# A log-sum-exp over 16384 rows: four-row reductions on VectorE, the last row loaded in two pieces, and a second pass in whole-ring operations

## Chip, cores, metric

One core of a Trainium2 chip. Times are device microseconds (us); the kernel before takes 168.85 us (median of 3 runs, 168.8 to 169.13). In the profile PE is TensorE, ACT is ScalarE, DVE is VectorE, SP is SyncE, which issues the DMAs here.

## The reference

```python
x = np.random.randn(32, 512, 1024).astype(np.float32)
def reference(x):
    max_x = np.max(x, axis=-1, keepdims=True)
    return (max_x.squeeze(-1) + np.log(np.sum(np.exp(x - max_x), axis=-1))).astype(np.float32)
```

The input is 67 MB, the output 64 KB. Each of the 128 partitions holds 128 rows of 1024 values ("a row" below is 128x1024, one row per partition, 512 KB).

## The kernel before

It computes ln(sum(exp(x))) without the maximum, checks that every sum lies inside wide bounds, and runs a second, exact pass only if one does not. On this input the second pass is never executed. The parts that matter, with cuts marked:

```python
RING = 48                                  # rows of input that fit in the ring
loads = [16, 16, 16, 16, 13, 10, 9, 7, 6, 5, 4, 3, 2, 2, 1, 1, 1]
ACCUMULATED_FROM = NC - 5                  # NC = 128
FIRST_CHECK = 112
# ... tiles; check(c0, c1, i, last): clamp the sums, count those that changed, add the count by matmul
for size in loads:
    p0 = c0 % RING
    nc.sync.dma_start(out=ring[:, p0 : p0 + size, :], in_=x_rows[:, c0 : c0 + size, :])
    if c0 >= ACCUMULATED_FROM:             # the last 5 rows: exp and sum in one ScalarE instruction
        for r in range(size):
            nc.scalar.activation(out=v, in_=v, func=AF.Exp, accum_out=sumexp[:, c0 + r : c0 + r + 1])
    else:                                  # four rows of exp, then one VectorE sum a row
        for b in range(0, size, 4):
            nc.scalar.activation(out=v, in_=v, func=AF.Exp)
            for r in range(b, b + s):
                nc.vector.scalar_tensor_tensor(out=lo, in0=lo, scalar=1.0, in1=ring[:, p0 + r, H:d],
                    op0=ALU.mult, op1=ALU.add, accum_out=sumexp[:, c0 + r : c0 + r + 1])
    if c0 < FIRST_CHECK <= c0 + size:      # the early ln
        nc.scalar.activation(out=res[:, 0:FIRST_CHECK], in_=sumexp[:, 0:FIRST_CHECK], func=AF.Ln)
        check(0, FIRST_CHECK, 0, False)
    c0 += size
nc.scalar.activation(out=res[:, FIRST_CHECK:NC], in_=sumexp[:, FIRST_CHECK:NC], func=AF.Ln)
nc.sync.dma_start(out=out_view, in_=res)
check(FIRST_CHECK, NC, 1, True)
nc.vector.tensor_copy(out=nbad, in_=count)
outside = nc.values_load(nbad[0:1, 0:1], ...)
with tc.If(outside > 0):                   # the second pass: 16 steps of 8 rows, two slots
    for k, c0 in enumerate(range(0, NC, 8)):
        # ... load 8 rows, negated max of 8 rows, then for each row:
        #     exp with the negated max as bias and the sum as accumulator (128 in all)
    # ... ln, subtract, store
```

## Time and profile before

| | before |
|---|---|
| time, median | 168.85 us |
| span of the profile | 167.0 us |
| last row has landed | 160.24 us |
| ScalarE's last accumulation ends | 162.07 us |
| output has landed | 163.88 us |

From the page: busy tenths in 40 slices of 4.2 us, packets of the instruction queue (packets, MB, share), the chain of waits by engine, and groups of instructions (line, engine, operation, shapes, count, busy us, mean ns, idle time before them and what ended it).

```profile
span 167.0 us, 438 instructions
...
DVE  0000005665077712776066746757737393584810
ACT  3000049990899519992599879989597979879980
...
DMA  7979998999799799989999999999999999999800
...
q14 instruction: 6, 0.05, 0.1%
...
DMA 73%; ACT 20%; DVE 3%; issue 1%; SPq 0%; PE 0%; ACTq 0%
...
L90 DVE SCALAR_TENSOR_TENSOR ring<-ring 128x512 f32<-128x512 f32 x123 | 77.6, 687 | 79.1 <-ACT ring L87 78.9
...
L96 ACT ACTIVATE res<-sumexp 128x112 f32<-128x112 f32 x1 | 0.3, 297 | 1.0 <-DVE ring L90 1.0
```

The DMA row is full to the end of slice 37: input streams without a break, and no compute engine is full all the way. The same from the view by windows (start and end, length, then busy time of PE, PEld, DVE, ACT, POOL, granted clock, share of the DMA engines, GB/s):

```profile
40.00:120.00 80.00, 0.00 (x0) 0.00 (x0) 44.83 (x141) 62.91 (x19) 0.00 (x0) 1.00 0.99 427
...
149.00:162.10 13.10, 0.19 (x2) 0.09 (x2) 6.91 (x26) 13.07 (x14) 0.00 (x0) 1.00 0.71 291
```

At 427 GB/s a row needs 1.23 us. In the last 13 us ScalarE is busy 13.07 of 13.10 us: there it looks like the limit. The timeline shows how it fell behind (start, length, engine, line, operation, in brackets the idle time before it):

```profile
143.01 4.56 ACT L87 ACTIVATE ring<-ring 128x4096 f32<-128x4096 f32 x2 [0.67 <-DMA ring<-in_x_dram]
148.62 0.30 ACT L96 ACTIVATE res<-sumexp 128x112 f32<-128x112 f32 x1 [1.04 <-DVE ring L90]
148.82 3.60 ACT L87 ACTIVATE ring<-ring 128x4096 f32<-128x4096 f32 x1
```

The early ln of 112 columns stands in ScalarE's queue behind the exp of rows 109 to 113 (counted from 0), waits 1.04 us for VectorE's sums of the first three of them, and holds the next exp up. And the end of the kernel:

```profile
160.94 1.04 ACT L80 ACTIVATE ring<-ring 128x1024 f32<-128x1024 f32 x1
161.88 0.18 ACT L80 ACTIVATION_READ_ACCUMULATOR ring<-ring 128x1 f32 x1
162.10 0.21 ACT L102 ACTIVATE res<-sumexp 128x16 f32<-128x16 f32 x1
...
162.34 0.35 SPq L103 DMA_DIRECT2D out_dram<-res  x1
...
162.77 0.14 DVE L105 CAST nbad<-count 1x1 int32<-1x1 f32 x1 [0.28 <-PE count L70]
```

The last work ends at 162.92 us, but the span goes to 167.0. SyncE's own waits in this last stretch (engine and line, what it waited for, us, times, longest; two of five lines) name one cause:

```profile
SPq L103 <- ACT res L102: 19.4, 1, 19.4
SPq L153 <- ACTq L111: 1.0, 1, 1.0
```

The second line: at the end of the program SyncE waited 1.0 us for ScalarE's sequencer at L111, which is the `tc.If`. The trace's records of the sequencers give the detail: ScalarE's compare-and-branch ends at 163.53 us and its next instruction comes at 166.22 us.

### The profile page before, as it was taken

The page shows a single profiled execution, that of the slowest core. Times are in us where ns is not written, and L with a number is a line of the kernel's source. Part 1 is how long each engine was busy: PE and PEld are TensorE (multiplying, and loading weights), DVE is VectorE, ACT ScalarE, POOL GpSimd, SP SyncE. Part 2 cuts the span into 40 slices and gives each one's busy share as a digit, 9 for nine tenths or more (in the row PEclk, how much of TensorE's full clock was granted, in tenths as well). Part 3 has the DMA queues.
Part 4 walks back from the last instruction along what each step waited for, and adds up shares of the span by engine and source line. Part 5 has one row for each costly group of instructions (what it writes and reads, how often), then busy time and mean ns, then how long its engine had stood idle before and what let it go on. Part 6 is the DMA issues. An engine that isn't in the chain of part 4 may idle for free.

```text
span 167.0 us, 438 instructions
## 1 busy us (share of the span) xinstructions
PE 0.4 (0%) x4; PEld 0.2 (0%) x4; DVE 78.8 (47%) x254; ACT 116.3 (70%) x48; POOL 0.2 (0%) x4
## 2 busy tenths in 40 slices
PE   0000000000000000000000000000000000000000
PEld 0000000000000000000000000000000000000000
DVE  0000005665077712776066746757737393584810
ACT  3000049990899519992599879989597979879980
POOL 0000000000000000000000000000000000000000
DMA  7979998999799799989999999999999999999800
GB/s 251 502 345 408 502 487 361 408 502 424 330 502 504 345 408 502 471 361 424 408 434 446 423 432 432 446 424 433 402 428 428 441 410 432 417 424 416 357 9 22
DMA packets 2598, 67.22 MB, mean 402 GB/s; under 512 B 288, under 2 KB 416, under 8 KB 800
## 3 DMA queue, kind: packets, MB, share of 16 engines
q1 hardware_dynamic: 2592, 67.18, 93.9%
q14 instruction: 6, 0.05, 0.1%
HBM read 67.11 MB, written 0.07 MB: 402 GB/s over the span
## 4 chain that ended last, share of the span: by engine, by line
DMA 73%; ACT 20%; DVE 3%; issue 1%; SPq 0%; PE 0%; ACTq 0%
DMA ring<-in_x_dram 73%; ACT ring L87 17%; ACT ring L80 3%; DVE ring L90 2%; SPq L76 0%; PE count L70 0%; DVE clamped L66 0%; DVE clamped L62 0%; DVE nbad L105 0%; ACTq L87 0%; ACT res L96 0%
## 5 line engine op out<-in xcount | busy, mean ns | idle before, releaser
L87 ACT ACTIVATE ring<-ring 128x4096 f32<-128x4096 f32 (+3 forms) x35 | 109.4, 3190 | 44.2 <-DMA ring<-in_x_dram 42.2
L90 DVE SCALAR_TENSOR_TENSOR ring<-ring 128x512 f32<-128x512 f32 x123 | 77.6, 687 | 79.1 <-ACT ring L87 78.9
L90 DVE DVE_READ_ACCUMULATOR ring<-ring 128x1 f32 x123 | 10.0, 81 | 0.0
L80 ACT ACTIVATE ring<-ring 128x1024 f32<-128x1024 f32 x5 | 5.2, 1039 | 0.0
L62 DVE TENSOR_SCALAR clamped<-sumexp 128x112 f32<-128x112 f32 (+1 forms) x2 | 0.4, 192 | 3.8 <-ACT ring L80 3.8
L57 ACT ACT_TABLE_LOAD x1 | 1.3, 1283 | 0.7 <-PEq L142 0.7
L96 ACT ACTIVATE res<-sumexp 128x112 f32<-128x112 f32 x1 | 0.3, 297 | 1.0 <-DVE ring L90 1.0
L80 ACT ACTIVATION_READ_ACCUMULATOR ring<-ring 128x1 f32 x5 | 0.9, 185 | 0.0
L70 PE MATMUL count<-ones,bad 128*1 128x1 f32 x4 | 0.4, 164 | 162.4 <-DVE clamped L66 162.4
L66 DVE SCALAR_TENSOR_TENSOR clamped<-clamped,sumexp 128x112 f32<-128x112 f32 (+1 forms) x2 | 0.5, 226 | 0.1
L58 DVE MEMSET ones<- 128x1 f32 x1 | 0.1, 59 | 0.8 <-PEq L142 0.8
L70 PEld LDWEIGHTS count<-ones,bad 128*1 128x1 f32 x4 | 0.2, 80 | 162.5 <-DVE clamped L66 162.5
L105 DVE CAST nbad<-count 1x1 int32<-1x1 f32 x1 | 0.1, 145 | 0.3 <-PE count L70 0.3
L102 ACT ACTIVATE res<-sumexp 128x16 f32<-128x16 f32 x1 | 0.2, 215 | 0.0
L66 DVE DVE_READ_ACCUMULATOR clamped<-clamped,sumexp 128x1 f32 x2 | 0.2, 82 | 0.0
L142 POOL MEMSET const-uint8-127<- 128x1 uint8 x1 | 0.1, 102 | 0.0
L142 POOL MEMSET const-bfloat16-1.0<- 128x1 bf16 x1 | 0.1, 101 | 0.0
L142 POOL MEMSET const-float32-0.0<- 128x1 f32 x1 | 0.1, 98 | 0.2 <-issue 0.2
L142 POOL MEMSET const-float32-1.0<- 128x1 f32 x1 | 0.1, 98 | 0.0
## 6 DMA issues: line engine op xcount, KB each, us to landing
ring<-in_x_dram SPq DMA_DIRECT2D x1, 6656.0 KB, 39.7
ring<-in_x_dram SPq DMA_DIRECT2D x1, 5120.0 KB, 38.1
ring<-in_x_dram SPq DMA_DIRECT2D x1, 4608.0 KB, 41.3
ring<-in_x_dram SPq DMA_DIRECT2D x1, 3584.0 KB, 39.0
ring<-in_x_dram SPq DMA_DIRECT2D x1, 3072.0 KB, 40.5
ring<-in_x_dram SPq DMA_DIRECT2D x1, 2560.0 KB, 40.8
ring<-in_x_dram SPq DMA_DIRECT2D x1, 2048.0 KB, 42.2
ring<-in_x_dram SPq DMA_DIRECT2D x2, 1024.0 KB, 44.9
```

The source lines that it names most:

```text
L57: nc.scalar.preload_act_table_set("natural_log_exp_and_others")
L58: nc.vector.memset(ones, 1.0)
L62: nc.vector.tensor_scalar(out=clamped[:, c0:c1], in0=sumexp[:, c0:c1], scalar1=LOW, scalar2=HIGH, op0=ALU.max, op1=ALU.min,)
L66: nc.vector.scalar_tensor_tensor(out=clamped[:, c0:c1], in0=clamped[:, c0:c1], scalar=0.0, in1=sumexp[:, c0:c1], op0=ALU.bypass, op1=ALU.n ...
L70: nc.tensor.matmul(count, lhsT=bad[:, i : i + 1], rhs=ones, start=i == 0, stop=last)
L80: nc.scalar.activation(out=v, in_=v, func=AF.Exp, accum_out=sumexp[:, c0 + r : c0 + r + 1])
L87: nc.scalar.activation(out=v, in_=v, func=AF.Exp)
L90: nc.vector.scalar_tensor_tensor(out=lo, in0=lo, scalar=1.0, in1=ring[:, p0 + r, H:d], op0=ALU.mult, op1=ALU.add, accum_out=sumexp[:, c0 + ...
L96: nc.scalar.activation(out=res[:, 0:FIRST_CHECK], in_=sumexp[:, 0:FIRST_CHECK], func=AF.Ln)
L102: nc.scalar.activation(out=res[:, FIRST_CHECK:NC], in_=sumexp[:, FIRST_CHECK:NC], func=AF.Ln)
L105: nc.vector.tensor_copy(out=nbad, in_=count)
L142: nc = _bacc.Bacc("TRN2", target_bir_lowering=False, num_devices=1)
```

## The change

Its intent: fewer VectorE instructions for the bulk rows, a shorter tail (only a quarter of the last row is left to do after the last byte lands; the two sums are joined because ln can add a per-partition bias before the logarithm), an early ln that waits for nothing recent, and a second pass of few, large instructions. Cut to its core:

```diff
-    loads = [16, 16, 16, 16, 13, 10, 9, 7, 6, 5, 4, 3, 2, 2, 1, 1, 1]
+    loads = [(16, "R")] * 5 + [(13, "T"), (10, "T"), (7, "T"), (5, "T"), (4, "T"), (3, "T"), (2, "T")]
+    loads += [(1, "A")] * 3
+    LAST = NC - 1
+    SPLIT = 3 * d // 4
+    EARLY = 80
@@ bulk rows
+            if how == "R":
+                nc.vector.reduce_sum(out=sumexp[:, c0 + b : c0 + b + s], in_=v, axis=AX.X)
+                continue
@@ early ln
-        if c0 < FIRST_CHECK <= c0 + size:
-            nc.scalar.activation(out=res[:, 0:FIRST_CHECK], in_=sumexp[:, 0:FIRST_CHECK], func=AF.Ln)
-            check(0, FIRST_CHECK, 0, False)
+        if size == 10:
+            nc.scalar.activation(out=res[:, 0:EARLY], in_=sumexp[:, 0:EARLY], func=AF.Ln)
@@ last row
+    load(p0, LAST, 1, 0, SPLIT)
+    load(p0, LAST, 1, SPLIT, d)
+    exp_sum(ring[:, p0, 0:SPLIT], LAST)
+    nc.scalar.activation(out=res[:, EARLY:LAST], in_=sumexp[:, EARLY:LAST], func=AF.Ln)
+    check(0, LAST, 0)
+    exp_sum(ring[:, p0, SPLIT:d], NC)
+    nc.scalar.activation(
+        out=res[:, LAST:NC], in_=sumexp[:, NC : NC + 1], func=AF.Ln, bias=sumexp[:, LAST:NC]
+    )
@@ second pass
-    with tc.If(outside > 0):
-        STEP = 8
-        for k, c0 in enumerate(range(0, NC, STEP)):
-            ...                       # load 8 rows, max of 8, 8 exps with bias and accumulator
+    with tc.If(outside > 0, preferred_fallthrough_block=False):
+        for c0 in range(0, NC, RING):
+            s = min(RING, NC - c0)
+            load(0, c0, s)
+            nc.vector.tensor_reduce(out=neg, in_=v, op=ALU.max, axis=AX.X, negate=True)
+            nc.vector.tensor_add(out=v, in0=v, in1=neg[:, :, None].to_broadcast([P, s, d]))
+            nc.scalar.activation(out=v, in_=v, func=AF.Exp)
+            nc.vector.reduce_sum(out=sumexp[:, c0 : c0 + s], in_=v, axis=AX.X)
```

("R": four rows by one reduction. "T": one pair-sum a row, as before. "A": exp with accumulator.) ScalarE's order in the built program differs in one place from the source: the ln of 47 columns comes ahead of the exp of the 768-column piece.

More of the change, by code (lines that the diff above doesn't have):

```diff
@@ L38 @@
     RING = 48
-    loads = [16, 16, 16, 16, 13, 10, 9, 7, 6, 5, 4, 3, 2, 2, 1, 1, 1]
-    ACCUMULATED_FROM = NC - 5
-    FIRST_CHECK = 112
-    assert sum(loads) == NC
+    loads = [(16, "R")] * 5 + [(13, "T"), (10, "T"), (7, "T"), (5, "T"), (4, "T"), (3, "T"), (2, "T")]
[3 more added lines that the diff above has]
+    EARLY = 80
+    assert sum(size for size, _ in loads) == LAST
     big = ctx.enter_context(tc.tile_pool(name="big", bufs=1))
@@ L48 @@
     ring = big.tile([P, RING, d], fp32, name="ring")
-    sumexp = stats.tile([P, NC], fp32, name="sumexp")
+    sumexp = stats.tile([P, NC + 1], fp32, name="sumexp")
     res = stats.tile([P, NC], fp32, name="res")
     clamped = stats.tile([P, NC], fp32, name="clamped")
-    bad = stats.tile([P, 2], fp32, name="bad")
+    bad = stats.tile([P, 4], fp32, name="bad")
     ones = stats.tile([P, 1], fp32, name="ones")
@@ L58, with add_to_count, check @@
     nc.vector.memset(ones, 1.0)
-    def check(c0, c1, i, last):
+    def add_to_count(i, last=False):
+        nc.tensor.matmul(count, lhsT=bad[:, i : i + 1], rhs=ones, start=i == 0, stop=last)
+    def check(c0, c1, i):
         nc.vector.tensor_scalar(
@@ L69, in check @@
         )
-        nc.tensor.matmul(count, lhsT=bad[:, i : i + 1], rhs=ones, start=i == 0, stop=last)
-    c0 = 0
-    for size in loads:
-        p0 = c0 % RING
-        assert p0 + size <= RING
-        nc.sync.dma_start(out=ring[:, p0 : p0 + size, :], in_=x_rows[:, c0 : c0 + size, :])
-        if c0 >= ACCUMULATED_FROM:
-            for r in range(size):
-                v = ring[:, p0 + r, :]
-                nc.scalar.activation(
-                    out=v, in_=v, func=AF.Exp, accum_out=sumexp[:, c0 + r : c0 + r + 1]
-                )
-        else:
-            for b in range(0, size, 4):
-                s = min(4, size - b)
-                v = ring[:, p0 + b : p0 + b + s, :]
-                nc.scalar.activation(out=v, in_=v, func=AF.Exp)
-                for r in range(b, b + s):
-                    lo = ring[:, p0 + r, 0:H]
-                    nc.vector.scalar_tensor_tensor(
-                        out=lo, in0=lo, scalar=1.0, in1=ring[:, p0 + r, H:d],
-                        op0=ALU.mult, op1=ALU.add,
-                        accum_out=sumexp[:, c0 + r : c0 + r + 1],
-                    )
-        if c0 < FIRST_CHECK <= c0 + size:
-            nc.scalar.activation(
-                out=res[:, 0:FIRST_CHECK], in_=sumexp[:, 0:FIRST_CHECK], func=AF.Ln
-            )
-            check(0, FIRST_CHECK, 0, False)
-        c0 += size
@@ L102, with load, exp_sum @@
-    nc.scalar.activation(out=res[:, FIRST_CHECK:NC], in_=sumexp[:, FIRST_CHECK:NC], func=AF.Ln)
-    nc.sync.dma_start(out=out_view, in_=res)
-    check(FIRST_CHECK, NC, 1, True)
+        add_to_count(i)
+    def load(p0, c0, size, k0=0, k1=d):
+        nc.sync.dma_start(
+            out=ring[:, p0 : p0 + size, k0:k1], in_=x_rows[:, c0 : c0 + size, k0:k1]
+        )
+    def exp_sum(v, c):
+        nc.scalar.activation(out=v, in_=v, func=AF.Exp, accum_out=sumexp[:, c : c + 1])
+    c0 = 0
+    p0 = 0
@@ new lines @@
+    for size, how in loads:
+        if p0 + size > RING:
+            p0 = 0
+        load(p0, c0, size)
+        for b in range(0, size, 4):
+            s = min(4, size - b)
+            v = ring[:, p0 + b : p0 + b + s, :]
+            if how == "A":
+                exp_sum(v, c0 + b)
+                continue
+            nc.scalar.activation(out=v, in_=v, func=AF.Exp)
+            if how == "R":
+                nc.vector.reduce_sum(out=sumexp[:, c0 + b : c0 + b + s], in_=v, axis=AX.X)
+                continue
+            for r in range(b, b + s):
+                lo = ring[:, p0 + r, 0:H]
+                nc.vector.scalar_tensor_tensor(
+                    out=lo, in0=lo, scalar=1.0, in1=ring[:, p0 + r, H:d],
+                    op0=ALU.mult, op1=ALU.add,
+                    accum_out=sumexp[:, c0 + r : c0 + r + 1],
+                )
+        c0 += size
+        p0 += size
+        if size == 10:
+            nc.scalar.activation(out=res[:, 0:EARLY], in_=sumexp[:, 0:EARLY], func=AF.Ln)
@@ new lines @@
+    load(p0, LAST, 1, 0, SPLIT)
[6 more added lines that the diff above has]
+        out=res[:, LAST:NC], in_=sumexp[:, NC : NC + 1], func=AF.Ln, bias=sumexp[:, LAST:NC]
+    )
+    nc.sync.dma_start(out=out_view, in_=res)
+    for i, c in ((1, LAST), (2, NC)):
+        nc.vector.tensor_scalar(
+            out=bad[:, 3:4], in0=sumexp[:, c : c + 1],
+            scalar1=LOW, scalar2=HIGH, op0=ALU.max, op1=ALU.min,
+        )
+        nc.vector.tensor_tensor(
+            out=bad[:, i : i + 1], in0=bad[:, 3:4], in1=sumexp[:, c : c + 1], op=ALU.not_equal
+        )
+        add_to_count(i, last=i == 2)
@@ L108 @@
         nbad[0:1, 0:1], min_val=0, max_val=P * NC,
-        skip_runtime_bounds_check_because="a count of sums"
+        skip_runtime_bounds_check_because="a count of sums",
     )
-    with tc.If(outside > 0):
-        STEP = 8
-        for k, c0 in enumerate(range(0, NC, STEP)):
-            p0 = (k % 2) * STEP
-            xt = ring[:, p0 : p0 + STEP, :]
-            neg = clamped[:, c0 : c0 + STEP]
-            nc.sync.dma_start(out=xt, in_=x_rows[:, c0 : c0 + STEP, :])
-            nc.vector.tensor_reduce(out=neg, in_=xt, op=ALU.max, axis=AX.X, negate=True)
-            for r in range(STEP):
-                v = ring[:, p0 + r, :]
-                nc.scalar.activation(
-                    out=v, in_=v, func=AF.Exp, bias=clamped[:, c0 + r : c0 + r + 1],
-                    accum_out=sumexp[:, c0 + r : c0 + r + 1],
-                )
-        nc.scalar.activation(out=res, in_=sumexp, func=AF.Ln)
+    with tc.If(outside > 0, preferred_fallthrough_block=False):
+        for c0 in range(0, NC, RING):
+            s = min(RING, NC - c0)
+            v = ring[:, 0:s, :]
+            neg = clamped[:, c0 : c0 + s]
+            load(0, c0, s)
+            nc.vector.tensor_reduce(out=neg, in_=v, op=ALU.max, axis=AX.X, negate=True)
+            nc.vector.tensor_add(out=v, in0=v, in1=neg[:, :, None].to_broadcast([P, s, d]))
+            nc.scalar.activation(out=v, in_=v, func=AF.Exp)
+            nc.vector.reduce_sum(out=sumexp[:, c0 : c0 + s], in_=v, axis=AX.X)
+        nc.scalar.activation(out=res, in_=sumexp[:, 0:NC], func=AF.Ln)
         nc.vector.tensor_sub(out=res, in0=res, in1=clamped)
```

## The prediction

> **What bounds it.** The windows view has the DMA engines 98 to 100% busy to 149 us: the loads never starve. By the trace's landing times a row of 128x1024 takes 1.21 to 1.24 us, and the last lands at 160.24 us. So 160 of 167.0 us is the input stream, which the change does not shorten. The chain of waits is 73% DMA, then from 143 us ScalarE: it never catches up again. In the timeline it loses 1.0 us at 148.6, where the early ln waits for VectorE sums just issued ("ACT res <- DVE ring 1.0"), then runs without a gap to 162.07, 1.8 us after the last landing. The last 5.0 us are ln (0.21), output DMA (1.5 to landing) and the end of the program. In it ScalarE passes its compare-and-branch at 163.53 and executes its next instruction only at 166.22; SyncE was through at 165.27. The instruction queue fetched 8 KB at 165.2. The Trainium skill ("Runtime: NRT & Kernel Launch", Instruction fetch mechanics) says that a taken branch whose target is outside the current window forces a fetch; this stall of 2.7 us agrees.
>
> **The change, costed.**
> 1. 80 rows in 20 reductions of 128x4096 in place of 80 sums of 512 pairs. A sum costs 0.614 us start to start, 2.46 per four rows. The skill ("VectorE: DVE Perf Modes", tier table) gives tensor_reduce one element per cycle only; from 0.96 GHz I estimate 4.3 to 4.4 us per four rows. That is slower than now, but under the 4.84 us in which four rows land: I estimate the fourth load issued at 44.4 us instead of 39.87, still 17 us before the queue runs dry. VectorE busy rises to about 115 us: 0 us on the path.
> 2. The early ln (80 columns) waits only for sums finished long before: removes the 1.0 us wait.
> 3. Fewer accumulated rows at 1.04 us, more in batches at 0.88: -0.2 us. The last row in two pieces costs ScalarE 0.83 + 0.40 instead of 1.04, and ln of 47 (0.25) now comes after the loads: about +0.3 us. ScalarE is still behind: by my sum it ends its accumulation at 161.0 to 162.0 (before 162.07). So the split gains almost nothing.
> 4. The last checks are as long as before.
> 5. Second pass: never executed, but 128 exps become 3, so the branch passes over few instructions. I expect ScalarE's stall to go, and SyncE to set the end: -1.0 to -1.4 us.
> 6. Fewer VectorE instructions: the fetch at 123.8 us, after which one DMA engine landed 0.95 us later, moves or goes; between -0.9 and 0.
>
> **Sum.** ScalarE's end -0.5, branch -1.3: about -1.8 us; 168.85 to 167.0 us, 80% range 166.1 to 168.3. Under 165.5 would need 3.4 us: faster 4%, same 95%, slower 1%.
>
> **What would show it.** Reductions of 4.3 us and no starved DMA slice; no wait of the early ln; ScalarE without a gap over the last 30 us; under 0.5 us between ScalarE's branch and next instruction; from the end of the last accumulation to the end 3.6 us instead of 5.0.
>
> **What would make it wrong.** Reductions at half rate (VectorE becomes the limit, over 180 us); a branch that still fetches (then 168.3); an instruction fetch that delays a DMA engine at the very end; pieces of 1 KB per partition that land late; ScalarE waiting for its own accumulator between the last exp and ln.

## The result

| | before | after |
|---|---|---|
| time, median | 168.82 us (4 runs, 168.63 to 169.13) | 166.32 us (4 runs, 166.22 to 166.67) |
| span of the profile | 167.0 us | 164.6 us |
| last row has landed | 160.24 us | 159.60 us |
| ScalarE's last accumulation ends | 162.07 us | 161.25 us |
| output has landed | 163.88 us | 163.15 us |
| ScalarE: end of last branch, next instruction | 163.53, 166.22 us | 163.25, 163.38 us |

The ratio is 0.9854 (95% interval 0.9833 to 0.9875), 2.5 us. Ratios in this document are from runs of a kernel and of the kernel before in the same rounds, and not quite the ratio of the medians; where microseconds are worked out from one it is multiplied by 168.8.

The page after, the same parts as before:

```profile
span 164.6 us, 297 instructions
...
DVE  0000004999789995999959998699998668665951
ACT  3000039990699709994299915998799999999992
...
DMA  7989998997998999899899899999998999999940
...
q14 instruction: 2, 0.02, 0.0%
...
DMA 66%; DVE 19%; ACT 12%; issue 1%; SPq 0%; PE 0%; ACTq 0%; DVEq 0%
...
L102 DVE TENSOR_REDUCE sumexp<-ring 128x4 f32<-128x4096 f32 x20 | 87.0, 4412 | 33.8 <-ACT ring L100 33.8
L106 DVE SCALAR_TENSOR_TENSOR ring<-ring 128x512 f32<-128x512 f32 x44 | 27.7, 688 | 8.8 <-ACT ring L100 8.7
```

The reductions take 4.41 us for four rows (4.33 start to start), more than the pair-sums did (2.46 us, four times 0.614 start to start), and VectorE is now nearly full for most of the stream. The DMA row did not suffer. The instruction queue moved 2 packets in place of 6. VectorE's 19% in the chain are the reductions that free ring space; the loads they release were issued over 28 us before they landed (for instance 117.30, landed 148.30), so the DMA engines never ran dry on account of them.

The end of the kernel after, in the timeline:

```profile
159.79 0.24 ACT L119 ACTIVATE res<-sumexp 128x47 f32<-128x47 f32 x1
...
159.94 0.83 ACT L86 ACTIVATE ring<-ring 128x768 f32<-128x768 f32 x1
...
160.76 0.40 ACT L86 ACTIVATE ring<-ring 128x256 f32<-128x256 f32 x1
...
161.07 0.19 ACT L86 ACTIVATION_READ_ACCUMULATOR ring<-ring 128x1 f32 x1
...
161.29 0.29 ACT L122 ACTIVATE res<-sumexp 128x1 f32<-128x1 f32 x1
...
161.61 0.35 SPq L125 DMA_DIRECT2D out_dram<-res  x1
...
161.97 0.15 DVE L137 CAST nbad<-count 1x1 int32<-1x1 f32 x1 [0.28 <-PE count L66]
```

The 256-column piece landed at 159.60 us and its exp started at 160.76: ScalarE was 1.2 us late, and the split bought no earlier start. SyncE's waits at the end, with no wait for ScalarE's sequencer among them:

```profile
SPq L125 <- ACT res L122: 13.3, 1, 13.3
SPq L181 <- PEq L181: 0.6, 2, 0.4
```

So the 2.42 us between the two spans are: 0.82 us from an earlier last accumulation (162.07 to 161.25), 0.09 us lost between it and the output's landing (1.81 to 1.90), and 1.69 us from the output's landing to the end (3.15 to 1.46). The question for the experiments is which part of the change made the first and the third.

One more reading from the trace is needed for the first. A load raises its semaphore 16 times, which is read here as once for each of the 16 DMA engines; it has landed with the last of them. The distance of the last from the one before it is how far one DMA engine lags. Beside it stand the fetches of 8 KB by the instruction queue while the input streams, and how many of VectorE's records (waits and accumulator reads included) had started by then:

```
kernel    8 KB fetches (VectorE records)   lag of one engine, by landing           last row landed: 15 engines, all
before    53.3 (54), 123.8 (185)           0.21 at 120.05, 1.16 at 129.52          159.10, 160.24
after     132.7 (57)                       0.07 at 128.33, 0.48 at 137.31          159.14, 159.60
```

(A third fetch before, at 158.9 us, 1.3 us before the last landing, left no mark on the lag.) Fifteen engines are as fast in both kernels. One falls behind just when a fetch comes into the stream, and in these two traces the lag stays to the end, presumably because all 16 are full to the end and none can catch up. (It isn't always so: in runs 1 and 7 the lag after the first fetch, 0.37 and 0.43 us, fell back to about 0.2 us.) That the fetches are VectorE's is inferred: the first comes after 54 to 61 of VectorE's records in every trace that has one in the stream, whether at 53 or at 133 us, and after 11 or 34 of ScalarE's.

The trace's records of single DMA packets (start, duration, size, but not the engine) show what a fetch does. A packet of the stream ends within 6 ns of the fetch's start, the next one starts 3 to 12 ns before the fetch's end, and that one runs long. In the changed kernel the fetch at 132.68 us takes 0.33 us and the packet of 28 KB that starts at 132.99 takes 1.73 us, where 1.06 is usual: one engine loses 0.33 + 0.66 = 0.99 us. There are 20 such fetches between 20 and 150 us in the 14 kept traces, and they lose 0.84 to 1.00 us each. Of the stream's packets of 20 to 64 KB between 20 and 158 us, exactly the 20 that follow a fetch run more than 0.4 us over the usual (median) time for their size, and run 8, which has no fetch there, has none.

The lag grows by all of that only if the engine that is hit was the last already. Before the fetch in the changed kernel the engines landed up to 0.93 us apart; by elimination the one that was hit stood 0.50 us before the last (127.83 and 128.33), which leaves 0.49 us of the 0.99, and the lag after is 0.48. At the second fetch of the kernel before it was the last engine that was hit: 0.21 + 0.99 = 1.20, and 1.16 was measured.

### The profile page after: what moved, and what is told of

Same layout as the page of the kernel before. It is cut to its first block, busy times and chain, and to the rows that moved or that the text cites. A ratio compares the mean times of both kernels' runs of the same rounds, so it can differ in the third digit from the quotient of the medians.

```text
span 164.6 us, 297 instructions
## 1 busy us (share of the span) xinstructions
PE 0.6 (0%) x6; PEld 0.3 (0%) x6; DVE 116.0 (70%) x117; ACT 116.4 (71%) x48; POOL 0.2 (0%) x4
## 4 chain that ended last, share of the span: by engine, by line
DMA 66%; DVE 19%; ACT 12%; issue 1%; SPq 0%; PE 0%; ACTq 0%; DVEq 0%
DMA ring<-in_x_dram 66%; DVE sumexp L102 19%; ACT ring L100 9%; ACT ring L86 2%; SPq L81 0%; DVE bad L133 0%; DVE bad L129 0%; ACT res L119 0%; PE count L66 0%; DVE nbad L137 0%; ACTq L100 0%; DVEq L129 0%; ACTq L119 0%
## 5 line engine op out<-in xcount | busy, mean ns | idle before, releaser
L100 ACT ACTIVATE ring<-ring 128x4096 f32<-128x4096 f32 (+3 forms) x34 | 110.1, 3304 | 44.4 <-DMA ring<-in_x_dram 44.2
L102 DVE TENSOR_REDUCE sumexp<-ring 128x4 f32<-128x4096 f32 x20 | 87.0, 4412 | 33.8 <-ACT ring L100 33.8
L106 DVE SCALAR_TENSOR_TENSOR ring<-ring 128x512 f32<-128x512 f32 x44 | 27.7, 688 | 8.8 <-ACT ring L100 8.7
L86 ACT ACTIVATE ring<-ring 128x1024 f32<-128x1024 f32 (+2 forms) x5 | 4.3, 869 | 0.0
L106 DVE DVE_READ_ACCUMULATOR ring<-ring 128x1 f32 x44 | 3.7, 83 | 0.0
```

The lines of the kernel that those rows point to most:

```text
L102: nc.vector.reduce_sum(out=sumexp[:, c0 + b : c0 + b + s], in_=v, axis=AX.X)
```

## The experiments

Twelve runs, in three groups. Kernels of a group ran on one chip in the same rounds, beside the kernel before. All twelve gave the right result.

### 1. The new second pass alone

The kernel before, with

```diff
-    with tc.If(outside > 0):
-        ...                                  # old second pass
+    with tc.If(outside > 0, preferred_fallthrough_block=False):
+        ...                                  # new second pass
```

> The kernel before with the changed kernel's second pass alone (never executed). Theory (the shorter second pass removes ScalarE's stall after its branch): ScalarE's next instruction comes under 0.7 us after its compare-and-branch instead of 2.7 us, last accumulation to the end of the span 3.3 to 3.6 us instead of 4.96, ScalarE's last accumulation still ends at 162.0 +- 0.3 us; time 167.2 us +- 0.3, 1.4 to 1.6 us under before. Rival (the 2.5 us come from the sums, the loads and the split; an unexecuted pass costs nothing): same time as before within 0.3 us.

Measured: 167.31 us (167.21 to 167.54), ratio 0.992 (0.9908 to 0.9933), 1.35 us. ScalarE's branch ends at 163.76 us, its next instruction comes at 163.88. The last accumulation ends at 162.15 us, as before, and the span 3.28 us later. In the kernel before the instruction queue fetches 8 KB twice during the stall, at 164.65 and 165.22 us; here it fetches nothing after 158.97 us. The theory holds, the rival falls: code that is never executed cost 1.35 us.

### 2. The changed kernel with the old second pass

The reverse edit on the changed kernel.

> The changed kernel with the old second pass put back. Theory: the stall of 2.7 us returns and the time is 1.2 to 1.6 us over the changed kernel's 166.3, so 167.6 to 167.9 us; last accumulation still at 161.2 +- 0.3 us. Rival: it stays at 166.3.

Measured: 167.90 us (167.68 to 168.37), ratio 0.9951 (0.9936 to 0.9965); against 0.9854 of the changed kernel, 1.6 us more. The branch ends at 162.85 us, the next instruction comes at 165.38: the stall is back. SyncE's wait for ScalarE's sequencer at the `tc.If` is back too:

```profile
SPq L185 <- ACTq L143: 0.8, 1, 0.8
```

The last accumulation ended at 161.31 us, unchanged. Removing the pass and restoring it agree: about 1.4 to 1.6 us of the 2.5 come from here.

### 3. The last row in one piece

The changed kernel, with

```diff
-    load(p0, LAST, 1, 0, SPLIT)
-    load(p0, LAST, 1, SPLIT, d)
-    exp_sum(ring[:, p0, 0:SPLIT], LAST)
-    nc.scalar.activation(out=res[:, EARLY:LAST], ...)
+    load(p0, LAST, 1)
     check(0, LAST, 0)
-    exp_sum(ring[:, p0, SPLIT:d], NC)
-    nc.scalar.activation(out=res[:, LAST:NC], ..., bias=sumexp[:, LAST:NC])
+    exp_sum(ring[:, p0, :], LAST)
+    nc.scalar.activation(out=res[:, EARLY:NC], in_=sumexp[:, EARLY:NC], func=AF.Ln)
```

and one check of a single column at the end in place of two.

> The changed kernel with the last row in one piece again (one exp, one ln of 48 columns after it). Theory: ScalarE is 0.7 us or more behind the landings in the tail, so the split only adds an instruction and an ln to the busy engine: the last accumulation ends at 160.8 us instead of 161.25 and the time is 0.3 to 0.6 us SHORTER than the changed kernel's (165.7 to 166.0). Rival, the intent of the change (the split shortens the tail): 0.3 to 0.8 us longer.

Measured: 166.09 us (165.63 to 166.12), ratio 0.9834 (0.982 to 0.9848). The last accumulation ends at 161.00 us. The direction is the theory's, but the interval overlaps that of the changed kernel, which ran in other rounds, so it was run again beside the changed kernel (6).

### 4. Pair-sums for all batched rows

The changed kernel, with

```diff
-    loads = [(16, "R")] * 5 + [(13, "T"), ...
+    loads = [(16, "T")] * 5 + [(13, "T"), ...
```

> The changed kernel with all batched rows summed by pairs again, no 4-row reduction: VectorE again has about 270 instructions. Theory (fewer VectorE instructions mean fewer instruction fetches on the input's DMA engines): two fetches of 8 KB come back inside the stream, one DMA engine lags the second slowest by about 1.1 us instead of 0.48, the last row lands at 160.1 to 160.3 us instead of 159.6, and the time is 0.3 to 0.8 us longer (166.6 to 167.1). Rival A (the reductions bring nothing, they are off the path): same time within 0.2 us and the last landing at 159.6. Rival B (VectorE at 70% busy delays things): faster than the changed kernel.

Measured: 167.22 us (167.21 to 167.28), ratio 0.9911 (0.9898 to 0.9924): 0.0057 of 168.8, 0.96 us more than the changed kernel, a little over the range expected. (The changed kernel ran in other rounds; run 3, in the same rounds as this one, took 166.09 us.) Fetches at 53.5 us (54 VectorE records) and 129.2 us (191); the lag grows from 0.02 to 0.38 us at the first and from 0.38 to 1.35 us at the second; the last row lands at 160.41 us and the last accumulation ends at 162.08 us, where the kernel before has it. Rival A, the reductions bring nothing, falls, and so does B: VectorE has less to do here, and the time is longer. Nor do pair-sums as such slow a DMA engine: VectorE made them from 62 to 128 us too, between the fetches, and the lag stayed at 0.37 to 0.38 us.

One doubt had to be cleared. In this build the early ln stands further ahead and waited 2.6 us at 117.6 us, so ScalarE's tail could have been late from that. The timeline says no:

```profile
149.20 8.27 ACT L100 ACTIVATE ring<-ring 128x4096 f32<-128x4096 f32 x3 [0.28 <-DMA ring<-in_x_dram]
```

ScalarE had caught up by then and stood waiting for the load that landed at 149.12 us. The changed kernel waits at the same place:

```profile
148.38 8.25 ACT L100 ACTIVATE ring<-ring 128x4096 f32<-128x4096 f32 x3 [0.27 <-DMA ring<-in_x_dram]
```

for a load that landed at 148.30 us. The landing is 0.82 us later, the start 0.82, the last accumulation 0.83.

This kernel is also before plus everything but the reductions, and it takes 167.22 us, while the new second pass alone gave 167.31. So the split, the early ln and the new load sizes together are worth about 0.1 us on top of the pass, which is within the intervals, and only as long as the two fetches are there.

### 5. The changed kernel again

> The changed kernel itself, beside the others of this call: 166.3 us +- 0.2, last landing 159.6 us, last accumulation 161.25 us.

Measured: 166.48 us (166.21 to 166.82), ratio 0.9851 (0.9835 to 0.9866); last landing 159.73, last accumulation 161.39 us. It repeats.

### 6. The last row in one piece, beside it

> The changed kernel with the last row in one piece, again, now on the same chip and in the same rounds as the changed kernel, since the earlier difference (0.2 us) was as large as the intervals. Theory (ScalarE is behind the landings, so the split costs an instruction and an ln): 0.2 to 0.4 us under the changed kernel. Rival (no effect): within 0.1 us. Rival (the split helps): 0.3 us or more over it.

Measured: 165.73 us (165.68 to 165.91), ratio 0.9806 (0.9793 to 0.982). This interval lies wholly below that of run 5; the quotient of the two ratios is 0.9954, 0.8 us. That is more than the 0.2 to 0.4 expected; with run 3 (0.9834) the gain lies between 0.3 and 0.8 us. The spans of the profiles differ by 0.62 us here (164.74 and 164.12). ScalarE's end in this kernel:

```profile
158.65 1.04 ACT L86 ACTIVATE ring<-ring 128x1024 f32<-128x1024 f32 x1
...
159.69 1.04 ACT L86 ACTIVATE ring<-ring 128x1024 f32<-128x1024 f32 x1
160.63 0.19 ACT L86 ACTIVATION_READ_ACCUMULATOR ring<-ring 128x1 f32 x1
160.85 0.24 ACT L119 ACTIVATE res<-sumexp 128x48 f32<-128x48 f32 x1
```

In the changed kernel's first profile the exp of the row before the last starts at the same time:

```profile
158.63 1.04 ACT L86 ACTIVATE ring<-ring 128x1024 f32<-128x1024 f32 x1
```

But the last accumulation ends at 160.82 us here, in place of 161.25 there and 161.39 in run 5. (The shorter check at the end plays little part: from the last accumulation to the end it is 3.30 us here and 3.35 in run 5.) The split put a ln between two exps and made one exp into two while ScalarE was late anyway. This version beats both kernels.

### 7. The early ln of 80 columns alone

The kernel before, with

```diff
-    nc.scalar.activation(out=res[:, 0:FIRST_CHECK], in_=sumexp[:, 0:FIRST_CHECK], func=AF.Ln)
+    nc.scalar.activation(out=res[:, 0:80], in_=sumexp[:, 0:80], func=AF.Ln)
     ...
-    nc.scalar.activation(out=res[:, FIRST_CHECK:NC], in_=sumexp[:, FIRST_CHECK:NC], func=AF.Ln)
+    nc.scalar.activation(out=res[:, 80:NC], in_=sumexp[:, 80:NC], func=AF.Ln)
```

> The kernel before with only the early ln cut to 80 columns instead of 112. Theory: the wait of 1.0 us for the sums just issued goes, ScalarE then waits for landings in the tail instead, the last accumulation ends at 161.2 to 161.5 us instead of 162.07 and the time is 0.5 to 0.9 us under before (167.9 to 168.2). Rival (the wait is slack that the landings give back): within 0.2 us of before.

Measured: 169.18 us (168.74 to 169.51), ratio 1.0 (0.9986 to 1.0014). My theory falls. The wait of 1.04 us is gone from the profile and the time is the same within 0.24 us. The timeline shows where it went:

```profile
148.46 8.28 ACT L87 ACTIVATE ring<-ring 128x4096 f32<-128x4096 f32 x3 [0.33 <-DMA ring<-in_x_dram]
157.10 1.06 ACT L80 ACTIVATE ring<-ring 128x1024 f32<-128x1024 f32 x1 [0.36 <-DMA ring<-in_x_dram]
```

ScalarE now waits for loads instead, last for the load of two rows that are accumulated singly. From there five rows at 1.04 us follow without a gap, whatever came before. In the kernel before that load landed at 156.49 us and ScalarE took it up at 156.78:

```profile
156.78 1.04 ACT L80 ACTIVATE ring<-ring 128x1024 f32<-128x1024 f32 x1
```

After the 1.0 us wait it was only 0.3 us late where the tail is decided, and 0.3 us was all there was to gain. (In this run's profile the whole stream landed 0.55 us later than in the one before, so that its end times, 160.79 and 162.40 us, are compared through their distance, 1.61 us against 1.83.)

This holds for the kernel before. The changed kernel with the old early ln was not run. There the loads land earlier, and ScalarE runs without a wait from 148.38 us to its last accumulation, so a wait of 1 us in that stretch might well have cost time.

### 8. Reductions nearly everywhere

The one-piece version of run 3, with

```diff
-    ... + [(13, "T"), (10, "T"), (7, "T"), (5, "T"), (4, "T"), (3, "T"), (2, "T")]
+    ... + [(13, "R"), (10, "R"), (7, "R"), (5, "R"), (4, "R"), (3, "T"), (2, "T")]
```

> The changed kernel, last row in one piece, and all batches but the last two (5 rows) summed by 4-row reductions, so that VectorE executes fewer instructions than the number at which it fetched at 132 us. Theory: no instruction fetch while the input streams; the slowest DMA engine lags the second slowest by under 0.2 us; the last row lands at 159.2 to 159.4 us, ScalarE's last accumulation ends at 160.6 to 160.8 us; time 165.6 to 165.9 us, below both kernels. Rival (VectorE, now with 4.4 us per four rows to the end, finishes its last sums after ScalarE and the ln waits): last accumulation unchanged but the ln after it later, time 166.2 or more.

Measured: 172.51 us (172.47 to 172.9), ratio 1.0218 (1.0203 to 1.0233): slower than both kernels. The rival was right about the time:

```profile
ACT res L119 <- DVE ring L106: 6.7, 1, 6.7
```

VectorE never stands idle after 104 us; its last reduction ends at 163.86 us and its last sum at 166.90, while ScalarE's last accumulation had ended at 160.26. I had let VectorE start on each late load as soon as ScalarE's exp was done and left out its backlog: the reduction of the first four rows of the five-row load could have started at 146.94 us, when their exp ended, and started at 154.00. But the theory's own numbers came out: no fetch while the input streams (the first is at 170.0 us), a lag of 0.08 us, last row landed at 159.02 us, last accumulation at 160.26 us, earlier than expected. Put together:

```
kernel      fetches in the stream   lag at the end   last row landed   last accumulation ends
pairs (4)   2                       1.37             160.41            162.08
before      2                       1.14             160.24            162.07
after       1                       0.47             159.60            161.25
mostly R    0                       0.08             159.02            160.26
```

(The fetch at 158.9 us in the kernel before is not counted. "Mostly R" has the last row in one piece, so its fair partner is run 6, one piece and one fetch: 0.43, 159.57 and 160.82 us. Both times are about 0.55 us earlier here.) The other traces agree: the last row lands at 160.24 to 160.79 us in the seven with two fetches and at 159.57 to 159.79 us in the six with one.

### 9 and 10. Order of the blocks, or length of the pass

Run 1 changed two things, the length of the second pass and the order of the blocks. Run 9 is the kernel before with the order alone, run 10 with the length alone:

```diff
 9:
-    with tc.If(outside > 0):
+    with tc.If(outside > 0, preferred_fallthrough_block=False):
         ...                                  # old second pass
10:
     with tc.If(outside > 0):
-        ...                                  # old second pass
+        ...                                  # new second pass
```

> The kernel before with only the order of the two blocks turned round: the path without a second pass now comes first, and then jumps over the old, long second pass. Theory (what matters is that the jump's target lies too far ahead to be in the engine's instruction memory): ScalarE still stalls 2.3 to 2.8 us, time within 0.3 us of before. Rival (the taken conditional branch itself costs it): ScalarE's next instruction under 0.7 us after the branch, time 1.3 to 1.6 us under before.

Measured: 168.83 us (168.75 to 169.0), ratio 1.0 (0.9984 to 1.0017). ScalarE's jump ends at 163.85 us, its next instruction comes at 166.31: the stall stays.

> The kernel before with the new, short second pass but the old order of the blocks. Theory (distance): no stall, under 0.7 us between ScalarE's branch and its next instruction, time 1.2 to 1.5 us under before, as with both. Rival (order of blocks): stall of 2.3 us or more stays, time as before.

Measured: 167.42 us (167.14 to 167.53), ratio 0.9914 (0.9897 to 0.9931), 1.45 us. ScalarE's branch ends at 163.88 us, its next instruction comes at 164.00. The length of the code jumped over is the cause, the order of the blocks is none.

### 11 and 12. What the new second pass costs when it runs

Both kernels with

```diff
-LOW, HIGH = 1e-15, 1e15
+LOW, HIGH = 1e4, 1e15
```

so that every sum counts as outside and the second pass is executed.

> The kernel before with the lower bound of the check set to 1e4, so that every row counts as out of range and the second pass runs; the result stays right. What does the change cost on inputs that need the second pass? Estimate for the old one: 16 steps of load, max and exp over two slots of 8 rows, by the durations seen about (9.8 + 2 + 8.8 + 9) / 2 = 15 us each, so 235 to 250 us more: 400 to 430 us in all.

Measured: 425.09 us (2 runs, 425.06 and 425.12).

> The changed kernel with the same bound of 1e4. Estimate: nothing overlaps in whole-ring operations; per 48 rows load 60, max 52, add 52, exp 41, sum 52 us, together about 257 us, twice, and 171 us for 32 rows: about 685 us more, 830 to 870 us in all, twice the kernel before when forced. Rival (whole-ring operations are no slower): 400 to 430 us.

Measured: 853.20 us (2 runs, 853.16 and 853.25), twice as long. The page of the kernel before, forced (each slice is 10.6 us):

```profile
DVE  0035446376656570393474573672861870881680
ACT  1085949498987893059267377287188078177377
...
DMA  9999999999999994945946838829829928928800
```

and of the changed kernel, forced (each slice is 21.3 us):

```profile
DVE  0788997300499993069700499994069702999078
ACT  0677799500000006930000000005930000000920
...
DMA  9999999799400000000299400000000296000000
```

In the old pass load, maximum and exp overlap; in the new one load, VectorE and ScalarE take turns, and VectorE has three passes over the data where the old one had one. The gain of 1.4 us was bought with 428 us on inputs that need the second pass.

## Why the prediction was right or wrong

The time, 166.32 us, lies in the range of 166.1 to 168.3 us, near its lower end, and "within 2%" was given 95%. The gain was put at 1.8 us and is 2.5. The largest term, the stall, was right in mechanism and size. That the total came out this near owes something to luck, since a term that was worth nothing (2) stood in for part of one that was booked too small (6). Point by point:

1. **"0 us on the path" for the reductions: right about VectorE's time, wrong about the step as a whole.** The duration (4.3 to 4.4 us expected, 4.41 measured), the fourth load's issue (44.4 us expected, 44.18 in the trace) and the unbroken stream were right. But the reductions do act on the critical path, through item 6.
2. **"Removes the 1.0 us wait": the failed step.** It was taken as a gain in ScalarE's end. Run 7 removed the wait alone from the kernel before and gained 0.0 us (within 0.24). The idle time was real; the tail starts from a later landing, and only the 0.3 us by which ScalarE was late at that landing could have been saved.
3. **"The split gains almost nothing", about +0.3 us for it: right in direction.** It costs 0.3 to 0.8 us (runs 3 and 6).
4. **The checks:** the distance from the last accumulation to the end of VectorE's last conversion is 0.85 us before and 0.87 after. As said.
5. **Second pass, -1.0 to -1.4 us: right, at the upper end or a little over.** 1.35 us added alone, 1.45 us by length alone, 1.6 us taken away from the changed kernel.
6. **"Between -0.9 and 0" for fewer VectorE instructions: the mis-sized term.** The sum booked about -0.5 us for ScalarE's end from items 2, 3 and 6 together; it was 0.82 us in the profile, and run 4 gives 0.96 us to the reductions alone. The mechanism was named, but credited with too little, and the rest of the gain in ScalarE's end was credited to the ln.

Of what the prediction said would be seen, one thing failed: ScalarE was not "without a gap over the last 30 us". It waited 0.27 us for the load that it took up at 148.38 us (and 0.38 us at 128.41, before that stretch). That it waits there at all is why the landing of one slow DMA engine shifts the end. From the last accumulation to the end it took 3.36 us (3.6 expected, 4.96 before).

Shown: the stall comes with the length of the second pass (1, 2, 9, 10); the reductions move the last landing and the time (4); each fetch takes 0.84 to 1.00 us from one DMA engine of the stream (the packets of all kept traces), and with no fetch there is no lag (8); the split costs time (6). Only argued: that it is the number of VectorE's instructions that sets when the fetch comes. Open: why the packet after a fetch runs 0.53 to 0.66 us long, and what the early ln is worth in the changed kernel. No single lag is exact either: run 3, with one fetch, ends with a lag of only 0.26 us, yet its last row lands at 159.76 us, because there the other engines were later too (159.50).

## What to carry to other kernels

Code that is never executed can cost time: keep a rarely taken block short enough that the jump over it stays near, but measure what the rare case then costs when it does run. In a kernel bound by its input stream look at the slowest of the 16 DMA engines at the last load, not at their mean, and look for instruction fetches in the stream, since each one took 0.84 to 1.00 us from one of those engines here; fewer instructions on the busiest engine moved them or removed them. Before you value an idle gap on an engine, look for the next place where it waits for something else; if it waits there already, or nearly, the gap is worth only the rest.

## What the Trainium skill lacked or had wrong

- "Runtime: NRT & Kernel Launch", Instruction fetch mechanics, says that a taken branch to a target outside the window forces a fetch and a stall; the trace agrees and adds the size that the page lacks: 2.5 to 2.7 us on ScalarE (163.53 to 166.22 us before, 163.85 to 166.31 in run 9), with two fetches of 8 KB inside it, and 0.12 us without a fetch where the block is short (run 10).
- The same section gives refills in 16 KiB blocks of 256 instructions. Here each fetch in the stream was a single packet of 8 KB, and the two of the kernel before came after 54 and 185 of VectorE's records, 131 apart.
- The same section calls the cost of such a crossing mostly hidden. VectorE's own work shows no stall (its pair-sums keep their 0.61 us start to start across the fetches), but one of the 16 DMA engines of the input stream lost 0.84 to 1.00 us at each; the page does not mention it.
- "VectorE: DVE Perf Modes", the tier table, gives tensor_reduce one element per cycle; 4.41 us for 4096 elements agrees. The page does not say that the sum of a row can be had at 0.614 us start to start by adding its two halves with an accumulator, against about 1.1 us a row (4.33 / 4) by reduction.
- "ScalarE: Activation LUTs", What ACT_TABLE_LOAD costs, puts the overlap of back-to-back activations at about 93 ns; 4096 elements took 3.60 us, 3.51 start to start, which agrees. It has no cost for an accumulator output: 1024 columns took 1.04 us start to start with one, 0.95 without (126.83 to 127.78 us after).
- "DMA: Bandwidth & Descriptors", Specifications, lists about 358 GB/s as the limit of HBM for one core, without a condition; this core, with nothing else running in the program, read 427 GB/s from 40 to 120 us. The same page's measured table (425 GB/s for 16 MB) and the note under it, which keeps 358 GB/s for two cores that stream at once, fit this run; the row alone misleads.
